# A conv norm centred on a pilot mean, three output chunks computed together, and inputs moved by 64 bytes

## The chip, the cores and the metric

The kernel runs on one core of a Trainium2 chip. The metric is the device time of one execution in microseconds (us); the time before is the median of three runs, 2594.8 (2594.53 to 2596.46). The engines are TensorE (PE, matmuls; PEld its weight loads), VectorE (DVE), ScalarE (ACT), GpSimd (POOL) and SyncE (SP), whose queue issues the DMAs.

## What is computed

Two transformer blocks on x of 256 tokens by 2048 features, fp32. Each is modulated by six vectors made from a conditioning vector c (2048 by 12288 weights per block). Only the first block's mixer is touched by the change:

```python
mod = silu(c) @ mod_w + mod_b                       # SH1, SC1, G1, SH2, SC2, G2
h = rms_norm(x, norm1_g) * (1 + sc1) + sh1
u = h @ w_in + b_in; a, gt = split(u); u = a * sigmoid(gt)      # conv_in
u = depthwise_conv(u, dw_w, width=31, causal) + dw_b
u = silu(layer_norm(u, ln_g, ln_b))                 # mean, then variance of u - mean
y = u @ w_out + b_out                               # conv_out
x = x + (1 + g1) * y
h = rms_norm(x, norm2_g) * (1 + sc2) + sh2
x = x + (1 + g2) * (square(relu(h @ w1)) @ w2)      # the MLP, d_ff = 8192
# then the second block: two kinds of attention, gates, a gated MLP, a last norm
```

## The kernel before

Features lie on the 128 partitions, in 16 blocks (KB) of 128, and the 256 tokens are the columns. Each fp32 product is made of three products in a rounded format: a number is split into a high and a low part, and high by high, low input by high weight, and high input by low weight are added in PSUM. A weight chunk (128 output features by 2048) is one DMA of 1 MB into one of four buffers `wf` (`load_w`); ACT casts each half to `wh` (L177) and DVE subtracts it for the low half `wl` (L180); two chunks of split halves can be held. `mm` (L191, L194) makes a chunk with a 512-column matmul (high weight by both parts of the input, which lie side by side) and a 256-column one; `mm_one` (L210) with three of 256 columns per block, 48 for a chunk, into half a PSUM bank. The mixer's two projections use `mm_one`, the rest `mm`.

The first block begins with SH1, SC1 and an early part of conv_in (blocks 0 to 5), bound by its DMAs, until about 140 us. Then comes the conv_in loop for blocks 6 to 15: two chunks for each, twenty turns in all. In a turn (`turn`) stand, after a chunk's matmuls: 1.1 steps of the modulation jobs G1, SC2, SH2 (`step`; a step of `mod_part_pe` loads 1 MB `wm` into one of the same four buffers and runs four matmuls, L286; sixteen of them, a transpose L293 and an addition L294 make a part), taps of the depthwise convolution, and mean rows (`into_mean`, L606: a matmul by 1/2048 that adds a finished block into the mean). The convolution of a block is done in one of three ways: on PE (`conv_pe`, L630 and L639, blocks 4, 10, 14, 15), on POOL (`conv_pool`, blocks 1, 3, 5, 7, 9, 12: ACT makes the product L654 into a ring of eight, POOL adds it L655), on DVE (`conv_dve`, the six others, 31 taps each in PSUM, L662 and L665). `TAPS` and `POOL_TAPS` say how many taps stand in a turn; two of the DVE taps stand ahead of each `wl` (`between`). What is left goes into a drain loop after the last turn (L765).

When all sixteen blocks have been added, the mean is copied (L776), subtracted from each block (L778, ten on DVE, six on POOL), and squared (L368); PE adds the squares into the variance (L369), and six steps of the modulation jobs stand between. Four rows on DVE after one on ACT (`rstd`, L337 to L342) make the reciprocal root. Up to there each engine's instructions are kept in the order of the program (`in_order`, closed by `pinned.close()`); behind it a scheduler orders them by a simulation. Then each block is multiplied by the root (L788), put through Silu (L790) and split into `s` (`uHL`), and conv_out's sixteen chunks follow, each with 1.2 steps of modulation. `flush` runs what is left of the jobs, `norm_to` makes the MLP's input, and the MLP starts with three chunks together.

Of the kernel before, what the change touches and what calls it, by code (L numbers as in the profile page):

```python
# [9 lines left out]
F32 = mybir.dt.float32  # L10
# [21 lines left out]
CONV_PACE = 1.1  # L32
LN_STEPS = 6
WOUT_PACE = 1.2
# [38 lines left out]
class Builder:  # L73
# [62 lines left out]
    def weights(self):  # L136

        a = self.a
        out = []
        for j in range(EARLY, 16):  # L140
            out += [(a["conv_in"][16 + j], 16, j not in NATIVE), (a["conv_in"][j], 16)]
        out += [(a["conv_out"][j], 16) for j in range(16)]
# [17 lines left out]
    def take(self):  # L160

        while self.plan and len(self.ahead) <= AHEAD:
            self.ahead.append(self.load_w(*self.plan.pop(0)))
        return self.ahead.pop(0)

# [222 lines left out]

    def actHL(self, tag):
        return self.big.tile([P, KB, 2, S], F32R, tag=tag, name=self.nm(tag))  # L390

# [66 lines left out]
    def build(self):  # L458
# [28 lines left out]
        nc.vector.tensor_copy(cpad[:, :, 0:1], sc[:, 0:16].unsqueeze(2))  # L487
        sel = self.keep([P, 1], "sel")
        nc.vector.memset(sel, 0.0)
# [12 lines left out]

        front = self.big.tile([P, 2 * KB * S], F32, tag="uHL", name="front")
        xn = front[:, :KB * S].rearrange("p (k t) -> p k t", t=S)
        h = self.actHL("hHL")
        a1 = self.keep([P, 16], "a1")
# [93 lines left out]
        clock = [0]  # L600
        late, summed = [], []

        def into_mean(now):
            for due, i in [t for t in late if t[0] <= now]:
                late.remove((due, i))
                nc.tensor.matmul(mean[:, :S], lhsT=self.ones_d, rhs=co[:, i], start=not summed,  # L606
                                 stop=(len(summed) == KB - 1))
                summed.append(i)

        def tap(i, j):  # L610
# [86 lines left out]
        for s in range(SLICES):  # L697
# [18 lines left out]
            else:  # L716
# [6 lines left out]
                prods = front[:, d0:d0 + NPROD * S].rearrange("p (n t) -> p n t", t=S)  # L723
                wdiag = front[:, d0 + NPROD * S:].rearrange("p (n t) -> p n t", t=4 * S)
                nc.vector.memset(us[:, :, :PAD], 0.0)
# [11 lines left out]
        self.pace(CONV_PACE)  # L737
        mean = self.aux()
# [31 lines left out]
        self.warm_rsqrt(sg[:, 0:1])  # L770

        while len(self.jobs) > 2:
            self.step(1)
        var = self.aux()
        mn = self.t1()
        nc.scalar.copy(mn, mean[:, :S])  # L776
        for kb in range(KB):
            (nc.gpsimd if kb % 8 in (2, 5, 7) else nc.vector).tensor_tensor(  # L778
                out=co[:, kb], in0=co[:, kb], in1=mn, op=ALU.subtract)
            self.sq_into(var[:, :S], co[:, kb], kb == 0, kb == KB - 1)  # L780
            if kb % 2:
                self.step(LN_STEPS / 8)
        r = self.rstd(var[:, :S])
        pinned.close()
        self.pace(WOUT_PACE)
        s = self.actHL("uHL")
        for kb in range(KB):
# [39 lines left out]
        for j in range(16):  # L827
            ps = self.mm_one(self.take(), s, KB)
            t = self.t1()
# [3 lines left out]
            self.square_sum(st[:, :S], x[:, j], j)  # L833
            self.step()
        self.flush()

# [283 lines left out]
```

## Time and profile before

| what | us |
|---|---|
| median of three runs | 2594.8 |
| the profiled execution | 2594.32 |
| its span on the core | 2592.5 |
| PE busy | 2527.7 (97%) |
| DVE busy | 1828.1 (71%) |
| ACT busy | 1323.5 (51%) |
| POOL busy | 152.1 (6%) |

The profile is of one execution; its own time stands 1.8 us above its span. A busy engine is one with an instruction under way. TensorE's matmuls are pipelined, so that the times of neighbours overlap and only the distance from start to start tells what one costs. The mean granted clock of PE over the span is 0.989 of full speed. In the rows below a tile's name stands left of the arrow and what it is made from right of it; "x10" is a count of neighbours in one row; in square brackets stands how long the engine had been idle and what released it.

### The profile page before, as it was taken

What the parts mean: (1) busy time and instruction counts of PE and PEld (TensorE: products, weight loads), DVE (VectorE), ACT (ScalarE), POOL (GpSimd) and SP (SyncE); (2) the same over time, 40 slices, a digit from 0 to 9 for tenths busy, and PEclk for the clock granted to TensorE, in tenths of its full rate; (3) what the DMA queues carried; (4) which work ended last, traced back from release to release, by engine and by line L of the source; (5) the groups of instructions that cost most, each with busy time, mean ns of one, the idle gap of its engine ahead of it and who ended that gap; (6) DMA issues with size and microseconds to landing.
All of it is one profiled execution on the core that took longest, in us unless ns stands there. A gap on an engine that the chain in (4) does not pass through costs nothing.

```text
span 2592.5 us, 38179 instructions
## 1 busy us (share of the span) xinstructions
PE 2527.7 (97%) x15340; PEld 2164.4 (83%) x15340; DVE 1828.1 (71%) x2546; ACT 1323.5 (51%) x2143; POOL 152.1 (6%) x190
## 2 busy tenths in 40 slices
PE   6999899999999999999999999999999999999997
PEld 4788668788888888887888888888788888888886
DVE  4377754777887888867976778786766556666566
ACT  4367654554554644655454554554544444444454
POOL 0068800000000000000000000000000000000000
PEclk8999999999999999999999999999999999999999
DMA  9967478778888887854654677775466666665553
GB/s 394 416 242 279 180 274 313 277 279 318 297 291 292 296 293 289 313 190 168 227 202 167 209 251 267 275 271 191 160 222 228 222 209 229 216 223 203 187 176 116
DMA packets 110338, 638.43 MB, mean 246 GB/s; under 512 B 16336, under 2 KB 16592, under 8 KB 51792
## 3 DMA queue, kind: packets, MB, share of 16 engines
q1 hardware_dynamic: 110160, 635.99, 68.7%
q8 instruction: 120, 1.97, 0.3%
q14 instruction: 58, 0.48, 0.0%
HBM read 633.85 MB, written 2.10 MB: 245 GB/s over the span
## 4 chain that ended last, share of the span: by engine, by line
PE 95%; DMA 2%; DVE 1%; ACT 1%; issue 0%; POOL 0%; SPq 0%; DVEq 0%; ACTq 0%; POOLq 0%
PE mm L191 51%; PE mm L194 27%; PE mm L210 8%; PE aux L286 2%; PE mm L573 2%; DMA slots<-in_mod_a_dram 1%; PE mm L753 1%; PE aux L530 1%; DMA front<-in_mod_a_dram 1%; PE aux L369 1%; PE mm L639 1%; PE aux L422 1%; PE aux L454 1%; PE aux L271 0%; PE aux L573 0%; DMA x<-in_xT_dram 0%
## 5 line engine op out<-in xcount | busy, mean ns | idle before, releaser
L191 PE MATMUL mm<-hHL,wh 128*128 128x512 f32 x3520 | 1243.1, 397 | 11.9 <-DVE hHL L380 11.9
L180 DVE TENSOR_TENSOR wl<-wf,wh 128x1024 fp32r<-128x1024 f32 (+1 forms) x794 | 965.9, 1219 | 356.5 <-ACT wh L177 333.6
L177 ACT CAST wh<-wf 128x1024 fp32r<-128x1024 f32 (+1 forms) x794 | 825.4, 1042 | 404.8 <-PE mm L191 240.1
L194 PE MATMUL mm<-hHL,wl 128*128 128x256 f32 x3520 | 960.9, 283 | 0.6 <-DVE wl L180 0.6
L191 PEld LDWEIGHTS mm<-hHL,wh 128*128 128x128 f32 x3520 | 652.6, 188 | 149.6 <-issue 8.9
L191 PE MATMUL mm<-uHL,wh 128*128 128x512 f32 x1984 | 691.4, 394 | 0.0
L194 PEld LDWEIGHTS mm<-hHL,wl 128*128 128x128 f32 x3520 | 663.7, 189 | 20.5 <-DVE wl L180 1.2
L194 PE MATMUL mm<-uHL,wl 128*128 128x256 f32 x1984 | 536.1, 282 | 0.0
L243 ACT COPY t<-mm 128x256 f32<-128x256 f32 x377 | 140.5, 373 | 588.2 <-PE mm L191 586.2
L191 PEld LDWEIGHTS mm<-uHL,wh 128*128 128x128 f32 x1984 | 364.5, 188 | 73.9
L194 PEld LDWEIGHTS mm<-uHL,wl 128*128 128x128 f32 x1984 | 372.9, 188 | 13.4
L265 DVE SCALAR_TENSOR_TENSOR acc<-wm,silu_c,acc 128x1024 f32<-128x1024 f32 x210 | 268.8, 1280 | 30.7 <-DMA wm<-in_w_ada_dram 26.9
L246 DVE TENSOR_TENSOR t<-mm,t 128x256 f32<-128x256 f32 x319 | 134.9, 423 | 181.1 <-ACT t L243 180.5
L655 POOL TENSOR_TENSOR room<-room,front 128x255 f32<-128x255 f32 (+9 forms) x180 | 146.6, 815 | 171.4 <-ACT front L654 158.4
L210 PE MATMUL mm<-hHL,wh 128*128 128x256 f32 x544 | 99.9, 286 | 0.0
L210 PE MATMUL mm<-uHL,wh 128*128 128x256 f32 x512 | 96.2, 288 | 0.7 <-DVE uHL L133 0.7
L210 PEld LDWEIGHTS mm<-uHL,wh 128*128 128x128 f32 x512 | 79.8, 191 | 16.4 <-issue 11.7
L210 PEld LDWEIGHTS mm<-hHL,wh 128*128 128x128 f32 x544 | 84.0, 189 | 6.9 <-issue 4.5
L191 PE MATMUL mm<-m,wh 128*128 128x512 f32 x256 | 89.5, 397 | 0.0
L665 DVE SCALAR_TENSOR_TENSOR mm<-room,vecs,mm 128x255 f32<-128x255 f32 (+9 forms) x180 | 84.7, 471 | 4.8
L654 ACT ACTIVATE front<-room,vecs 128x255 f32<-128x255 f32 (+9 forms) x180 | 74.7, 487 | 7.9 <-POOL room L655 7.9
L210 PE MATMUL mm<-hHL,wl 128*128 128x256 f32 x272 | 76.7, 282 | 0.0
(174 smaller groups left out, 1776.1 us busy)
## 6 DMA issues: line engine op xcount, KB each, us to landing
wf<-in_w_dram SPq DMA_DIRECT2D x128, 1024.0 KB, 6.7
wm<-in_w_ada_dram SPq DMA_DIRECT2D x96, 1024.0 KB, 5.2
wf<-in_win_dram SPq DMA_DIRECT2D x68, 1024.0 KB, 5.0
wm<-in_mod_w_dram SPq DMA_DIRECT2D x64, 1024.0 KB, 5.8
wf<-in_wg_dram SPq DMA_DIRECT2D x44, 1024.0 KB, 5.0
wf<-in_wu_dram SPq DMA_DIRECT2D x44, 1024.0 KB, 4.8
wf<-in_wd_dram SPq DMA_DIRECT2D x32, 896.0 KB, 4.6
slots<-in_mod_a_dram SPq DMA_DIRECT2D x22, 1024.0 KB, 15.0
```

The source lines that it names most:

```text
L177: self.nc.scalar.copy(wh, w[:, k0:k0 + n, :])
L180: self.nc.vector.tensor_tensor(out=wl, in0=w[:, k0:k0 + n, :], in1=wh, op=ALU.subtract)
L191: self.nc.tensor.matmul(ps, lhsT=h, rhs=full, start=first, stop=last, skip_group_check=True)
L194: self.nc.tensor.matmul(ps[:, :S], lhsT=l, rhs=x[:, 0, :], start=False, stop=False, skip_group_check=True)
L210: self.nc.tensor.matmul(ps[:, :S], lhsT=a, rhs=x[:, k, b], start=(k == 0 and i == 0), stop=(k == nk - 1 and i == 2))
L243: nc.scalar.copy(tb, ps[:, S:])
L246: nc.vector.tensor_tensor(out=s, in0=ps[:, :S], in1=tb, op=ALU.add)
L265: nc.vector.scalar_tensor_tensor(out=acc, in0=w[:, i], scalar=cvec[:, k + i:k + i + 1], in1=acc, op0=ALU.mult, op1=ALU.add)
L286: nc.tensor.matmul(row[32 * j:32 * j + 32, :], lhsT=cpad[:, k], rhs=w[:, j * 512:(j + 1) * 512], start=(k == 0), stop=(k == KB - 1), skip_ ...
L654: nc.scalar.activation(pr, u[:, PAD:PAD + S - s], AF.Identity, scale=tap(i, j))
L655: nc.gpsimd.tensor_tensor(out=dst[:, s:], in0=dst[:, s:], in1=pr, op=ALU.add)
L665: nc.vector.scalar_tensor_tensor(out=acc[:, s:], in0=u[:, PAD:PAD + S - s], scalar=tap(i, j), in1=acc[:, s:], op0=ALU.mult, op1=ALU.add)
```

## The change

- *Taps.* `TAPS` goes from 8 to 10 and `POOL_TAPS` from 8 to 9; block 10 moves from PE to DVE.
- *Norm.* When eight blocks are in the mean, ACT copies it, times two, into `pilot`. From then on each turn and each iteration of the drain takes up to two finished blocks, subtracts the pilot (DVE) and squares (ACT), and PE adds the square to `var`, which shares a PSUM tile with the mean. At the end dm = mean − pilot, the variance is var − dm², and dm is subtracted from the blocks (ten on DVE, six on POOL).
- *Modulation.* One step stands in each iteration of the drain, `FILL` = 6 after it, and then what is left of SC2; only SH2 is left for conv_out.
- *conv_out.* Its first three chunks are loaded without a split; four of their halves are split ahead of the normalising loop, two inside it; the three chunks' matmuls (`product`) stand in that loop, block by block, in three PSUM tiles. The next chunk is asked for at the first of the three outputs, and the order is kept by `in_order` until the third.
- *64 bytes.* `h` of the first block and `s` begin 16 floats into their buffers, which get 32 floats more; the other inputs begin where their buffers do. `sel` is kept at 32 floats.

```diff
-LN_STEPS = 6
+FILL = 6
+PILOT = 8
-PE_CONV = (4, 10, 14, 15)
+PE_CONV = (4, 14, 15)
+SHIFT = 16
+SPARE = 32
-TAPS = 8
-POOL_TAPS = 8
+TAPS = 10
+POOL_TAPS = 9
...
-    def actHL(self, tag):
-        return self.big.tile([P, KB, 2, S], F32R, tag=tag, name=self.nm(tag))
+    def actHL(self, tag, shift=0):
+        t = self.big.tile([P, KB * 2 * S + SPARE], F32R, tag=tag, name=self.nm(tag))
+        return t[:, shift:shift + KB * 2 * S].rearrange("p (k a t) -> p k a t", a=2, t=S)
...
                 summed.append(i)
+                if len(summed) == PILOT:
+                    nc.scalar.activation(pilot, mean[:, :S], AF.Identity, scale=float(KB) / PILOT)
+
+        def centre():
+            if len(summed) < PILOT or centred[1] == len(summed):
+                return
+            i = summed[centred[1]]
+            centred[1] += 1
+            nc.vector.tensor_tensor(out=co[:, i], in0=co[:, i], in1=pilot, op=ALU.subtract)
+            sq = self.t1()
+            nc.scalar.activation(sq, co[:, i], AF.Square)
+            squares.append(sq)
+
+        def into_var():
+            while squares:
+                centred[0] += 1
+                nc.tensor.matmul(var[:, :S], lhsT=self.ones_d, rhs=squares.pop(0), start=False,
+                                 stop=(centred[0] == KB), skip_group_check=True)
...
         def turn():
             clock[0] += 1
             self.step()
+            into_var()
             taps(dve=TAPS - 4, pool=POOL_TAPS, pe=1)
             into_mean(clock[0])
+            centre()
+            centre()
...
             turn()
+            if i == KB - 1:
+                first = [self.take(ahead=0)]
             glu(i, ps[:, :S], sg)
...
             taps(pe=1, dve=6, pool=4)
+            self.step(1)
             into_mean(clock[0])
+            into_var()
+            centre()
+            centre()
...
+        dm = self.t1()
+        nc.vector.scalar_tensor_tensor(out=dm, in0=pilot, scalar=-1.0, in1=mean, op0=ALU.mult, op1=ALU.add)
+        d2 = self.t1()
+        nc.vector.tensor_tensor(out=d2, in0=dm, in1=dm, op=ALU.mult)
+        v = self.t1()
+        nc.vector.tensor_tensor(out=v, in0=var, in1=d2, op=ALU.subtract)
+        self.step(FILL)
         while len(self.jobs) > 2:
             self.step(1)
-        (the copy of the mean, sixteen subtractions, squares, variance rows and six steps)
+        r = self.rstd(v)
         for kb in range(KB):
+            (nc.gpsimd if kb >= 10 else nc.vector).tensor_tensor(out=co[:, kb], in0=co[:, kb], in1=dm,
+                                                                 op=ALU.subtract)
         self.pace(WOUT_PACE)
-        s = self.actHL("uHL")
+        s = self.actHL("uHL", SHIFT)
...
+        ws = first + [self.take(), self.take(ahead=0)]
+        parts = [half(ws[0], 0), half(ws[1], 0), half(ws[2], 0), half(ws[0], 8)]
+        pss = [self.mmps() for i in range(3)]
...
             self.split(s[:, kb, 0], s[:, kb, 1], t)
+            if kb < 8:
+                for i in range(3):
+                    product(i, parts[i], kb)
+            else:
+                product(0, parts[3], kb)
+                if kb == 9:
+                    parts += [half(ws[1], 8), half(ws[2], 8)]
+                for k in {9: (), 10: (8, 9), 11: (10, 11)}.get(kb, (kb,) if kb > 11 else ()):
+                    for i in (1, 2):
+                        product(i, parts[3 + i], k)
...
-            ps = self.mm_one(self.take(), s, KB)
+            ps = pss[j] if j < 3 else self.mm_one(self.take(), s, KB)
...
             self.step()
+            if j == 0:
+                self.ask(1)
+            if j == 2:
+                pinned.close()
```

How it moves the instructions is seen at three places. First PE at the end of the mean (L606 before, L613 now). Before, the variance rows (L369) follow in pairs, with a load's matmuls (L286, `wm`) between:

```order
L606 MATMUL aux_1223<-room,ones_d 128x256 x3
L369 MATMUL aux_3242<-t_292_3246,ones_d 128x256
L369 MATMUL aux_3242<-t_293_3250,ones_d 128x256
L369 MATMUL aux_3242<-t_294_3254,ones_d 128x256
L369 MATMUL aux_3242<-t_295_3258,ones_d 128x256
L286 MATMUL aux_2752<-wm_3261,cpad 32x512 x4
L369 MATMUL aux_3242<-t_297_3268,ones_d 128x256
L369 MATMUL aux_3242<-t_298_3272,ones_d 128x256
L286 MATMUL aux_2752<-wm_3275,cpad 32x512 x4
```

Now most variance rows (L634) stand further up; behind the last two come five loads' matmuls in a row (L292), SC2's transpose (L299), and then the first of the three chunks (L844), whose high weight meets both parts of the input and whose low weight the high part:

```order
L292 MATMUL aux_2779<-wm_3296,cpad 32x512 x4
L613 MATMUL aux_1223<-room,ones_d 128x256 x2
L634 MATMUL aux_1223<-t_303_3304,ones_d 128x256
L634 MATMUL aux_1223<-t_305_3311,ones_d 128x256
L292 MATMUL aux_2779<-wm_3320,cpad 32x512 x4
L292 MATMUL aux_2779<-wm_3326,cpad 32x512 x4
L292 MATMUL aux_2779<-wm_3332,cpad 32x512 x4
L292 MATMUL aux_2779<-wm_3338,cpad 32x512 x4
L292 MATMUL aux_2779<-wm_3344,cpad 32x512 x4
L299 MATMUL aux_3352<-const,t_314_3350 128x128 x4
L844 MATMUL mm_3404<-uHL_3383,wh_3388 128x256 x2
L844 MATMUL mm_3404<-uHL_3383,wl_3389 128x256
```

What stood between the variance rows now stands in one piece ahead of conv_out, and the variance rows are gone from there. Second, DVE behind its last tap (L665 before, L692 now). Before, the subtractions of the mean (L778) and the root (L338 to L342) follow directly, then the multiplication (L788):

```order
L665 SCALAR_TENSOR_TENSOR mm_3106<-room,vecs,mm_3106 128x226
L778 TENSOR_TENSOR room<-room,t_291_3243 128x256 x10
L338 TENSOR_SCALAR t_314_3345<-aux_3242 128x256
L339 TENSOR_TENSOR t_316_3347<-t_315_3346 128x256
L340 SCALAR_TENSOR_TENSOR t_316_3347<-t_316_3347,t_314_3345 128x256
L342 SCALAR_TENSOR_TENSOR t_317_3352<-t_316_3347,t_315_3346 128x256
L788 TENSOR_TENSOR room<-room,t_317_3352 128x256 x12
L133 TENSOR_TENSOR uHL_3354<-t_319_3356,uHL_3354 128x256
```

Now the last centrings (L626) come, dm, its square and the variance (L816 to L820), then SC2's addition (L300), the root (L344 to L348), ten subtractions of dm (L826) and the first chunk's low half (L136):

```order
L626 TENSOR_TENSOR room<-room,pilot 128x256 x2
L816 SCALAR_TENSOR_TENSOR t_306_3314<-pilot,aux_1223 128x256
L818 TENSOR_TENSOR t_307_3316<-t_306_3314 128x256
L820 TENSOR_TENSOR t_308_3318<-aux_1223,t_307_3316 128x256
L300 TENSOR_TENSOR mods<-aux_3352,vecs 128x16
L344 TENSOR_SCALAR t_316_3358<-t_308_3318 128x256
L345 TENSOR_TENSOR t_318_3360<-t_317_3359 128x256
L392 SCALAR_TENSOR_TENSOR a_4620<-mods,vecs 128x16
L346 SCALAR_TENSOR_TENSOR t_318_3360<-t_318_3360,t_316_3358 128x256
L348 SCALAR_TENSOR_TENSOR t_319_3365<-t_318_3360,t_317_3359 128x256
L826 TENSOR_TENSOR room<-room,t_306_3314 128x256 x10
L136 TENSOR_TENSOR wl_3389<-wf_2973,wh_3388 128x1024
```

An addition that needs the whole of SC2 stands ahead of the root, and the subtractions behind it. Third, PE at the start of the MLP, before (L286 and L293 belong to SH2; `hHL` is the MLP's input):

```order
L286 MATMUL aux_3865<-wm_4601,cpad 32x512 x4
L286 MATMUL aux_3865<-wm_4607,cpad 32x512 x4
L293 MATMUL aux_4615<-const,t_488_4613 128x128 x4
L191 MATMUL mm_4731<-hHL_4623,wh_4520 128x512
L194 MATMUL mm_4731<-hHL_4623,wl_4521 128x256
L191 MATMUL mm_4731<-hHL_4623,wh_4520 128x512
L194 MATMUL mm_4731<-hHL_4623,wl_4521 128x256
```

and now (L370 is the last row of the norm's sum of squares):

```order
L216 MATMUL mm_4565<-uHL_3383,wl_4488 128x256
L370 MATMUL aux_3641<-t_488_4617,ones_d 128x256
L197 MATMUL mm_4730<-hHL_4622,wh_4557 128x512
L200 MATMUL mm_4730<-hHL_4622,wl_4558 128x256
L197 MATMUL mm_4731<-hHL_4622,wh_4702 128x512
L200 MATMUL mm_4731<-hHL_4622,wl_4703 128x256
L197 MATMUL mm_4730<-hHL_4622,wh_4557 128x512
L200 MATMUL mm_4730<-hHL_4622,wl_4558 128x256
```

SH2's last steps are gone from there, and two chunks (`mm_4730`, `mm_4731`) alternate from the first block, where one stood alone.

## Rows read from the trace of the kernel before

**Rows 1.** The page's part 4: the chain that ended last, by engine.

```profile
PE 95%; DMA 2%; DVE 1%; ACT 1%; issue 0%; POOL 0%; SPq 0%; DVEq 0%; ACTq 0%; POOLq 0%
```

**Rows 2.** The view by stretch, two stretches; its second line names the columns.

```profile
core 0: us, PE busy (x) PEld busy (x) DVE busy (x) ACT busy (x) POOL busy (x), PEclk, DMA share, GB/s
311.00:319.00 8.00, 1.35 (x5) 0.80 (x4) 3.13 (x7) 5.42 (x12) 6.64 (x11) 0.66 0.00 0
338.00:361.00 23.00, 19.53 (x120) 13.62 (x113) 16.78 (x40) 18.89 (x41) 0.00 (x0) 0.85 0.57 215
```

**Rows 3.** The chain of waits, end of conv_in: start us, us, what.

```profile
296.81 1.77 PE mm L630 x32
...
299.24 3.48 PE mm L639 x53
...
327.49 1.06 PE aux L369 x4
```

**Rows 4.** DVE's groups by line, conv_in loop, 140 to 297 us.

```profile
L665 DVE SCALAR_TENSOR_TENSOR mm<-room,vecs,mm 128x255 f32<-128x255 f32 (+9 forms) x149 | 70.1, 470 | 3.8
L180 DVE TENSOR_TENSOR wl<-wf,wh 128x1024 fp32r<-128x1024 f32 x36 | 48.7, 1360 | 27.6 <-ACT wh L177 27.4
```

**Rows 5.** The timeline of POOL: start us, us, engine, line, operation, count.

```profile
159.56 24.89 POOL L655 TENSOR_TENSOR room<-room,front 128x244 f32<-128x244 f32 x29
...
205.79 29.29 POOL L655 TENSOR_TENSOR room<-room,front 128x229 f32<-128x229 f32 x32 [1.44 <-ACT front L654]
...
304.12 14.31 POOL L655 TENSOR_TENSOR room<-room,front 128x245 f32<-128x245 f32 x20 [0.41 <-ACT front L654]
```

**Rows 6.** The page's part 6: DMA issues, median us to landing last.

```profile
wm<-in_mod_w_dram SPq DMA_DIRECT2D x64, 1024.0 KB, 5.8
```

**Rows 7.** The timeline from the root to the first product.

```profile
338.19 0.42 DVE L338 TENSOR_SCALAR t<-aux 128x256 f32<-128x256 f32 x1 [10.55 <-ACT t L337]
...
340.00 4.12 DVE L788 TENSOR_TENSOR room<-room,t 128x256 f32<-128x256 f32 x12
...
343.25 0.58 PE L210 MATMUL mm<-uHL,wh 128*128 128x256 f32 x1
```

**Rows 8.** The timeline of PE in conv_out, the loads' matmuls.

```profile
366.85 1.07 PE L286 MATMUL aux<-wm,cpad 128*32 128x512 f32 x8
...
380.62 1.07 PE L286 MATMUL aux<-wm,cpad 128*32 128x512 f32 x8
```

**Rows 9.** The timeline, end of conv_out and start of the MLP.

```profile
458.17 0.28 PE L210 MATMUL mm<-uHL,wl 128*128 128x256 f32 x1
...
464.38 1.07 PE L286 MATMUL aux<-wm,cpad 128*32 128x512 f32 x8 [0.77 <-DMA wm<-in_mod_w_dram]
...
466.85 0.17 DVE L294 TENSOR_TENSOR mods<-aux,vecs 128x16 f32<-128x16 f32 x1 [0.53 <-PE aux L293]
...
489.49 0.37 ACT L243 COPY t<-mm 128x256 f32<-128x256 f32 x1 [4.33 <-PE mm L191]
```

**Rows 10.** The timeline at the next seam of this kind.

```profile
1199.47 0.40 PE L191 MATMUL mm<-uHL,wh 128*128 128x512 f32 x1
...
1225.84 0.64 ACT L243 COPY t<-mm 128x256 f32<-128x256 f32 x2
```

**Rows 11.** The timeline of DVE, low halves at the MLP's start.

```profile
477.51 4.63 DVE L180 TENSOR_TENSOR wl<-wf,wh 128x1024 fp32r<-128x1024 f32 x4
```

**Rows 12.** The timeline of PE, 512-column matmuls: 13 rows with hHL, 14 with m.

```profile
1104.30 0.40 PE L191 MATMUL mm<-hHL,wh 128*128 128x512 f32 x1
...
1108.51 0.40 PE L191 MATMUL mm<-hHL,wh 128*128 128x512 f32 x1
...
1814.26 0.39 PE L191 MATMUL mm<-m,wh 128*128 128x512 f32 x1
...
1818.85 0.40 PE L191 MATMUL mm<-m,wh 128*128 128x512 f32 x1
```

**Rows 13.** The timeline of PE, 256 columns: twelve matmuls from first to last.

```profile
440.00 0.40 PE L210 MATMUL mm<-uHL,wh 128*128 128x256 f32 x2
...
441.42 0.40 PE L210 MATMUL mm<-uHL,wh 128*128 128x256 f32 x2
```

More of the change, by code (lines that the diff above doesn't have):

```diff
@@ L141, in weights @@
             out += [(a["conv_in"][16 + j], 16, j not in NATIVE), (a["conv_in"][j], 16)]
-        out += [(a["conv_out"][j], 16) for j in range(16)]
+        out += [(a["conv_out"][j], 16, j >= 3) for j in range(16)]
         for g in range(4):
@@ L158, in weights, with take, ask @@
         return out
-    def take(self):
-        while self.plan and len(self.ahead) <= AHEAD:
+    def take(self, ahead=AHEAD):
+        self.ask(ahead + 1)
+        return self.ahead.pop(0)
+    def ask(self, n):
+        while self.plan and len(self.ahead) < n:
             self.ahead.append(self.load_w(*self.plan.pop(0)))
-        return self.ahead.pop(0)
     def load_w(self, src, nk=16, parted=True):
@@ L487, in build @@
         nc.vector.tensor_copy(cpad[:, :, 0:1], sc[:, 0:16].unsqueeze(2))
-        sel = self.keep([P, 1], "sel")
+        sel = self.keep([P, 32], "sel")[:, :1]
         nc.vector.memset(sel, 0.0)
@@ L500, in build @@
         SH1, SC1, G1, SH2, SC2, G2 = range(6)
-        front = self.big.tile([P, 2 * KB * S], F32, tag="uHL", name="front")
+        front = self.big.tile([P, 2 * KB * S + SPARE], F32, tag="uHL", name="front")
         xn = front[:, :KB * S].rearrange("p (k t) -> p k t", t=S)
-        h = self.actHL("hHL")
+        h = self.actHL("hHL", SHIFT)
         a1 = self.keep([P, 16], "a1")
@@ L600, in build @@
         clock = [0]
-        late, summed = [], []
+        late, summed, squares, centred = [], [], [], [0, 0]
         def into_mean(now):
@@ L606, in into_mean @@
                 nc.tensor.matmul(mean[:, :S], lhsT=self.ones_d, rhs=co[:, i], start=not summed,
-                                 stop=(len(summed) == KB - 1))
+                                 stop=(len(summed) == KB - 1), skip_group_check=True)
                 summed.append(i)
+                if len(summed) == PILOT:
[14 more added lines that the diff above has]
+                                 stop=(centred[0] == KB), skip_group_check=True)
         def tap(i, j):
@@ L723, in build @@
                 prods = front[:, d0:d0 + NPROD * S].rearrange("p (n t) -> p n t", t=S)
-                wdiag = front[:, d0 + NPROD * S:].rearrange("p (n t) -> p n t", t=4 * S)
+                wdiag = front[:, d0 + NPROD * S:d0 + 16 * S].rearrange("p (n t) -> p n t", t=4 * S)
                 nc.vector.memset(us[:, :, :PAD], 0.0)
@@ L737, in build @@
         self.pace(CONV_PACE)
-        mean = self.aux()
+        both = self.aux()
+        mean, var = both[:, :S], both[:, S:]
+        pilot = self.tp.tile([P, S], F32, tag="rs", bufs=1, name="pilot")
         self.between = lambda: taps(dve=2)
@@ L767, in build, with half, product @@
             taps(pe=1, dve=6, pool=4)
+            self.step(1)
             into_mean(clock[0])
+            into_var()
+            centre()
+            centre()
         into_mean(1 << 20)
         self.warm_rsqrt(sg[:, 0:1])
+        while centred[0] < KB:
+            into_var()
+            centre()
+            centre()
+        dm = self.t1()
[5 more added lines that the diff above has]
+        self.step(FILL)
         while len(self.jobs) > 2:
             self.step(1)
-        var = self.aux()
-        mn = self.t1()
-        nc.scalar.copy(mn, mean[:, :S])
+        r = self.rstd(v)
         for kb in range(KB):
[L778 to L784, printed above, removed]
-        self.pace(WOUT_PACE)
-        s = self.actHL("uHL")
+            (nc.gpsimd if kb >= 10 else nc.vector).tensor_tensor(out=co[:, kb], in0=co[:, kb], in1=dm,
+                                                                 op=ALU.subtract)
+        self.pace(WOUT_PACE)
+        s = self.actHL("uHL", SHIFT)
+        def half(w, k0):
+            wh = self.sp.tile([P, 8, P], F32R, tag="wh", name=self.nm("wh"))
+            wl = self.sp.tile([P, 8, P], F32R, tag="wl", name=self.nm("wl"))
+            self.split(wh, wl, w[:, k0:k0 + 8, :])
+            return wh, wl
+        ws = first + [self.take(), self.take(ahead=0)]
+        parts = [half(ws[0], 0), half(ws[1], 0), half(ws[2], 0), half(ws[0], 8)]
+        pss = [self.mmps() for i in range(3)]
+        def product(i, part, k):
+            h, l = part[0][:, k % 8, :], part[1][:, k % 8, :]
+            for n, (w, b) in enumerate(((h, 0), (h, 1), (l, 0))):
+                nc.tensor.matmul(pss[i][:, :S], lhsT=w, rhs=s[:, k, b], start=(k == 0 and n == 0),
+                                 stop=(k == KB - 1 and n == 2))
         for kb in range(KB):
```

## The prediction

> **What bounds the kernel now.** I read the chain of waits first: 95% of the span is TensorE (PE) [rows 1]. So only PE work removed, or a place where PE stands still, moves the time. The table by stretch shows such a place: from 311 to 319 us PE works 1.35 of 8 us, at a granted clock of 0.66, and the DMA queues carry nothing; from 338 to 361 its clock is 0.85 [rows 2]. The reader should see that this is the seam between the two projections of the conv mixer. A second seam lies at the MLP's start. The rest is a solid row of matmuls, on which only the part on alignment can act. All times below are us of the profiled execution. T0 = 296.81 is where the conv_in loop's last matmul ends and block 14's convolution on PE begins [rows 3]. Everything up to the end of the MLP's first three chunks, 489.49, when ScalarE (ACT) copies the last of the three out [rows 9], is compared with the same point after the change; what follows is the same work.
>
> **Step 1, the conv_in loop.** Block 10 leaves PE: its two parts are like those of block 14, 1.77 and 3.48 us [rows 3], so 5.2 us go. Ten of the sixteen variance rows come in: two blocks took 1.06 us in the tail [rows 3], 0.53 each, so 5.3 us. They cancel. VectorE (DVE) now gives 6 taps a turn and 2 before each low half. By the counts of the loop (36 halves, 20 turns) that is 9.6 taps of 70.1/149 = 0.47, 1.8 halves of 1.36 [rows 4], half a gate and half a centring, each about as long as a tap: 7.4 of the (297 − 140) / 20 = 7.85 us that a turn lasts. It fits by 0.4, but unevenly over the turns; a stall of 0 to 3 us, and I take 1. T0' = 297.8.
>
> GpSimd (POOL) is tighter. Nine products a turn leave it 7.85 / 9 = 0.87 us each. Before, it took 29 in 24.89 (0.86) and 32 in 29.29 (0.92), but 20 in 14.31 (0.72) in the drain, where DVE only added taps in PSUM [rows 5]. "SBUF — State Buffer", section "SBUF: two separate sides", of the Trainium skill says that a DVE instruction with two SBUF inputs and a GpSimd one shut each other out for a whole instruction; the 0.72 against 0.92, and low halves of 1.36 in the loop, agree with it. By that rule the ten centrings in the loop (two SBUF inputs) would hold POOL for some 4 us more. I keep it for the rival below.
>
> **Step 2, from T0' to the first product of conv_out.** Before, that took 46.4 us, to 343.25 [rows 7]. Now eleven loads of SC2 remain after T0', each of 1 MB, and DVE's order puts SC2's last addition in front of the reciprocal root (the second piece of order above), so the products wait for the loads. Three buffers serve them, since the first conv_out chunk holds the fourth. Three loads are under way at T0'; every later one waits for the matmuls of the load three before it, and lands 5.8 after its issue [rows 6]. On PE these matmuls are queued behind blocks 14 and 15 (5.2 each) and the last two means, which wait for DVE's last tap, about T0' + 20 (31 taps of 0.47, eight centrings, two weight diagonals). If nothing else is late, the last two loads are issued at T0' + 22 and 24 and consumed by T0' + 30. If ACT, whose copies for block 14 stand behind nine products, waits out a POOL backlog of up to 8, it is T0' + 38. I take T0' + 35, nearer the late end, since POOL has no slack in step 1: 332.8. Then:
> - from the end of the last load's matmuls to the addition, 466.85 + 0.17 less 464.38 + 1.07 = 1.6 [rows 9]: 334.4
> - four DVE rows of the root, 338.19 to 340.00 = 1.8 [rows 7]: 336.2
> - ten subtractions at 4.12 / 12 = 0.34 [rows 7]: 339.6
> - four low halves, 4.6 [rows 11]: 344.2
> - multiply, table load, Silu, split: 343.25 − 340.00 = 3.25 [rows 7]: 347.5, which is 4.2 later than before.
>
> The sixteen subtractions and square rows that stood in the tail are hidden by the loads; were the loads early, the chain would still hold DVE's 20 us of taps, so the cover is worth at most the 30 to 38 just bounded.
>
> **Step 3, three chunks together.** 144 matmuls at 1.42 / 12 = 0.118 [rows 13] are 17.0. The second halves of chunks 2 and 3 can be split only once the first halves of chunk 1 are done, at block 9: two casts and two low halves, which the two late blocks of chunk 1 cover in part; 0 to 4, I take 2. The restart runs at a lower clock, as the 0.85 of 338 to 361 shows: 15% of the first 15 us or so, 2.3. So 347.5 + 21.3 = 368.8. Before, the third chunk was done at 366.85, where its load's matmuls follow [rows 8]: 1.9 sooner. The normalising loop was PE's pace before and costs little; now it is covered, but later.
>
> **Step 4, thirteen chunks.** A chunk with one load's matmuls takes (380.62 − 366.85) / 2 = 6.89 [rows 8], thirteen 89.5; three more loads of SH2 at 1.07 [rows 9] are 3.2: 461.5. Before, the last matmul of conv_out ended at 458.17 + 0.28 = 458.45 [rows 9], and five loads' matmuls still lay behind it.
>
> **Step 5, the seam to the MLP.** Before, 458.45 to 489.49: 31.0, with the last load's wait and its matmuls until 465.45 [rows 9] and only one weight chunk split, so that four low halves stand at 477.51 [rows 11]. After, no load stands there and two chunks are interleaved from the first block. Then it should be like the next seam of this kind, 1199.87 to 1225.84 = 26.0 [rows 10]. 461.5 + 26.0 = 487.5, against 489.49: 2.0 sooner.
>
> **Step 6, 64 bytes.** 2160 matmuls of 256 columns (by the code 33 chunks of 48 in the two projections and 12 of 48 in the early one) read inputs moved by 64 bytes against the weights. No row shows such a pair. The nearest are the 512/256 pairs: (1108.51 − 1104.30) / 12 = 0.351 with hHL, in phase with its weights, (1818.85 − 1814.26) / 13 = 0.353 with m, 64 bytes off [rows 12]. The difference of 2.3 ns per pair may belong to either matmul and, for the 256 columns, to either sign: ± 2.3 ns × 2160 = ± 5 us. No reason excludes a side; I take 0. The spare bytes also move every buffer, but inputs of the 5760 pairs (360 full chunks of 16) stay where they were relative to weights in steps of 128 bytes: 0, bounded by ± 2.3 ns × 5760 = ± 13 us.
>
> The sum is −2.0 on 2594.3 (the span of 2592.5 and 1.8 around it); the median of the runs is 0.5 above that execution: 2592.8, so 2593.
>
> **The rivals.**
> - Slower: POOL can't take nine products a turn. At 0.92 each a turn lasts 8.3; ACT's casts wait behind its products, and once the one chunk of lead is gone PE waits 0.4 × 20 = 8 us in the loop. It decides from a mean spacing above 0.87. For it: the 0.92; against: the 0.86, and POOL ends sooner afterwards. 2593 + 8 = 2601.
> - Faster: POOL keeps up, the loads are done at T0' + 30 (−5), no late halves (−2) and a shorter clock ramp (−1.5): 2584.5. For it: the queues are idle from 311 to 319, so that transfers that wait for nothing but buffers have room; against: three buffers.
> - The phase is worth something by itself, −3 ns or so: −5 to −8, 2586; or the whole layout is worse, +8 to +13, 2604. Rows 12 show that 64 bytes matter by 0.7% at all.
> - A floor is gone. Matmuls of 256 columns are 118.3 ns apart [rows 13], which is more than 256 columns at 2.4 GHz, the full granted clock, would take (106.7). If the phase alone kept them there, up to 2160 × 11.6 ns = 25 us would go: 2568. "TensorE: Matmul & The Clock Gate", section "Back-to-back issue gap", of the Trainium skill gives the columns at 2.4 GHz and 2.5 ns, 109.2, for such a matmul by itself, and says that a stream with weight loads is set by both; by it the gain would be 20 us. The pairs with m, off phase, are no faster, which speaks against the floor.
>
> **How the numbers follow.** Runs differ by 0.1%, and about 0.2%, 5.2 us, is what can be told from no change. The forecast has 0.42, POOL's rival 0.20, the faster chain 0.20, a gain by phase or layout 0.09, a worse layout 0.04, the floor 0.05. Faster is 0.34 (0.20 + 0.09 + 0.05), slower 0.24, the rest 0.42. The range, 2581 to 2603, holds POOL's rival and the faster chain with some spread, and leaves out the floor and most of the bad layout.
>
> **What would show it.** Step 1: PE busy through the loop and its end within 2 us of 297.8; a gap before conv_in matmuls that ends with ACT or DVE would show the rival. Step 2: the last load's matmuls at 328 to 336, then the addition of SC2, the root and ten subtractions in a row on DVE, first product near 347.5. Step 3: three tiles alternating, 21 us. Step 5: 26 us. Step 6: the spacing of 118.3 ns and that of the pairs, either moved. The prediction is wrong if the spacing moves by over 2 ns, if the first product comes before 342 or after 353, or if a stretch after 490 changes.

## The result, and the profile after

The changed kernel takes 2618.41 us (median of four runs, 2617.36 to 2619.08) against 2594.66 before: a ratio of 1.0090, with a 95% interval of 1.0072 to 1.0107. It is 23.8 us slower; 2593 with a range to 2603 was forecast. The chain of the profile after shows at once that PE no longer sets the time as it did in [rows 1]:

```profile
PE 90%; DMA 3%; DVE 3%; ACT 2%; POOL 1%; issue 0%; SPq 0%; POOLq 0%; DVEq 0%; ACTq 0%
```

The table below gives, for the kernels of this study, when the work came past five places. The loop's end is the end of the last modulation matmul ahead of block 14's convolution; the first product is the start of conv_out's first matmul; then come the ends of its third and of its sixteenth chunk, of the 48th pair of the MLP (three chunks), and of the span. Each is the start or end of one matmul record of that kernel's profile, counted from the start of its span.

| us | loop end | first product | third chunk | conv_out | MLP's three | span |
|---|---|---|---|---|---|---|
| before | 296.8 | 343.3 | 366.9 | 458.5 | 489.8 | 2592.5 |
| after | 304.9 | 358.2 | 390.8 | 484.1 | 511.9 | 2617.3 |
| e1_pool8 | 297.2 | 354.0 | 386.6 | 479.9 | 507.4 | 2612.9 |
| e2_dve8 | 305.0 | 379.1 | 411.7 | 498.8 | 526.6 | 2631.2 |
| e3_norm_ahead | 304.0 | 356.4 | 386.4 | 479.7 | 507.4 | 2612.0 |
| e4_fill_late | 303.4 | 345.5 | 378.1 | 486.2 | 513.8 | 2618.3 |
| e5_noshift | 304.6 | 357.1 | 389.7 | 484.2 | 511.7 | 2616.8 |
| e6_before_phase | 297.5 | 344.2 | 367.5 | 456.4 | 487.8 | 2590.5 |
| e7_skew | 303.1 | 354.9 | 378.4 | 471.6 | 499.6 | 2604.5 |
| e8_taps_skew_root | 296.9 | 349.6 | 374.1 | 466.3 | 493.8 | 2598.2 |
| e9_fill1_layout | 298.0 | 346.2 | 368.9 | 464.4 | 491.9 | 2594.4 |
| e10_layout | 306.0 | 358.7 | 391.3 | 482.2 | 510.3 | 2613.3 |

The differences of neighbouring columns, after less before, make up the 24.8 us between the two spans, but for rounding: the end of the conv_in loop +8.1, from there to the first product +6.8, the three chunks +8.9 (32.6 for 23.7), the other thirteen +1.8, the seam to the MLP −3.6, and all that follows +2.7. The loop itself lasted 10.0 us longer, since its first chunk started 1.9 us sooner in the profile after (138.3, for 140.2 before). Over the twelve profiles that start lies between 137.9 and 140.2; why is open.

The loop first. POOL's additions, which answer to [rows 5], now stand almost without a gap:

```profile
149.92 69.78 POOL L682 TENSOR_TENSOR room<-room,front 128x251 f32<-128x251 f32 x77
...
247.83 38.66 POOL L682 TENSOR_TENSOR room<-room,front 128x237 f32<-128x237 f32 x45 [2.43 <-ACT front L681]
```

77 in 69.78 are 0.91 us each. Twenty turns from 138.3 to 304.9 are 8.33 us each, nine times 0.93. The chain runs over POOL here, from a product of ACT through additions, back into a product, and then into the cast of a weight half (start, us, what):

```profile
193.44 1.52 ACT front L681 x4
195.00 0.60 POOL room L682
...
212.20 0.49 ACT front L681
213.05 0.94 ACT wh L183
214.02 1.39 DVE wl L186
```

PE feels it at two places. Its waits from 140 to 305 us were one of 0.2 us before; now they are these (us in total, times, longest):

```profile
PE aux L299 <- ACT t L296: 5.9, 1, 5.9
PE aux L292 <- DMA wm<-in_mod_w_dram: 4.0, 1, 4.0
```

The 4.0 us, until 225.4, are for a modulation load that was issued at 218.1, behind the weight halves of the chain above. The 5.9 us, until 268.7, are for ACT's copy ahead of the transpose of G1. That copy stands behind products that wait for POOL, and then behind instructions that are themselves part of the change: the pilot, and the squares of two blocks that wait for DVE's centrings (`in_order` keeps ACT to that order):

```profile
263.87 0.28 ACT pilot L618
264.17 1.29 DVE room L626 x2
265.48 0.42 ACT t L628
...
266.25 1.88 ACT wh L183 x2
268.13 0.49 ACT t L296
```

After each of the two stops PE first goes on at a granted clock of 0.50 (225.3 to 230.0, and 268.6 to 271.0). The view by stretch shows the second stop, in the first row, which before was

```profile
240.00:280.00 40.00, 40.00 (x335) 33.76 (x334) 29.87 (x50) 29.50 (x60) 36.16 (x45) 1.00 0.64 230
```

and then PE nearly still at the seam, at half clock (a granted clock of 0.50, 1.2 GHz), while the DMA engines too are idle for 44% of that time:

```profile
240.00:280.00 40.00, 34.07 (x241) 28.66 (x240) 32.78 (x59) 28.94 (x61) 34.36 (x43) 0.91 0.51 185
340.00:360.00 20.00, 5.03 (x23) 2.54 (x20) 10.58 (x23) 8.14 (x11) 0.00 (x0) 0.50 0.56 209
360.00:380.00 20.00, 13.96 (x74) 11.34 (x73) 9.42 (x21) 10.96 (x21) 0.00 (x0) 0.84 0.08 26
```

The columns are those of [rows 2]. The chain of the seam, which answers to [rows 3, 7], shows what stands there:

```profile
334.30 7.74 DMA wm<-in_mod_w_dram
...
342.09 1.98 PE aux L292 x8
...
345.88 0.17 DVE mods L300
...
347.76 3.10 DVE room L826 x9
350.86 4.54 DVE wl L136 x4
...
355.82 1.28 ACT L850
357.12 0.61 ACT t L850
357.75 0.41 ACT uHL L135
...
358.18 0.42 DVE uHL L136
358.61 0.35 DVE room L848
...
358.98 0.61 ACT t L850
```

First the last loads of SC2, then its addition, the root, the subtractions and the low halves, as step 2 had them. Behind them a round of four that repeats: Silu on ACT (0.61), cast on ACT (0.41), subtraction on DVE (0.42), the next block's multiplication on DVE (0.35), 1.86 us from Silu to Silu. At full clock PE does the nine matmuls of a block in 1.1 us and waits for the next; in the first three blocks and again behind the second halves, at a granted clock of 0.50, they stand 0.213 us apart and take about as long as the round.

### The profile page after: what moved, and what is told of

Its sections match the earlier page's. It is cut to its first block, busy times and chain, and to the rows that moved or that the text cites. A ratio compares the mean times of both kernels' runs of the same rounds, so it can differ in the third digit from the quotient of the medians.

```text
span 2617.3 us, 38011 instructions
## 1 busy us (share of the span) xinstructions
PE 2528.2 (97%) x15244; PEld 2163.3 (83%) x15244; DVE 1850.2 (71%) x2595; ACT 1327.1 (51%) x2141; POOL 151.3 (6%) x190
## 4 chain that ended last, share of the span: by engine, by line
PE 90%; DMA 3%; DVE 3%; ACT 2%; POOL 1%; issue 0%; SPq 0%; POOLq 0%; DVEq 0%; ACTq 0%
PE mm L197 51%; PE mm L200 26%; PE mm L216 5%; DMA slots<-in_mod_a_dram 2%; PE mm L580 2%; PE aux L292 1%; POOL room L682 1%; DMA wm<-in_mod_w_dram 1%; PE aux L537 1%; DMA front<-in_mod_a_dram 1%; PE mm L785 1%; PE aux L429 1%; PE aux L461 1%; DVE wl L186 0%; PE aux L277 0%
## 5 line engine op out<-in xcount | busy, mean ns | idle before, releaser
L197 PEld LDWEIGHTS mm<-uHL,wh 128*128 128x128 f32 x1984 | 364.7, 188 | 78.1 <-DVE uHL L136 0.3
L271 DVE SCALAR_TENSOR_TENSOR acc<-wm,silu_c,acc 128x1024 f32<-128x1024 f32 x210 | 268.7, 1280 | 27.5 <-DMA wm<-in_w_ada_dram 17.9
L692 DVE SCALAR_TENSOR_TENSOR mm<-room,vecs,mm 128x255 f32<-128x255 f32 (+14 forms) x210 | 98.9, 471 | 5.9
L681 ACT ACTIVATE front<-room,vecs 128x255 f32<-128x255 f32 (+9 forms) x180 | 77.0, 488 | 14.1 <-POOL room L682 14.0
L216 PE MATMUL mm<-uHL,wh 128*128 128x256 f32 x416 | 75.9, 282 | 0.0
L216 PEld LDWEIGHTS mm<-uHL,wh 128*128 128x128 f32 x416 | 63.9, 188 | 8.4 <-issue 6.7
```

The costliest lines, as they stand in the source:

```text
L197: self.nc.tensor.matmul(ps, lhsT=h, rhs=full, start=first, stop=last, skip_group_check=True)
L216: self.nc.tensor.matmul(ps[:, :S], lhsT=a, rhs=x[:, k, b], start=(k == 0 and i == 0), stop=(k == nk - 1 and i == 2))
L271: nc.vector.scalar_tensor_tensor(out=acc, in0=w[:, i], scalar=cvec[:, k + i:k + i + 1], in1=acc, op0=ALU.mult, op1=ALU.add)
L681: nc.scalar.activation(pr, u[:, PAD:PAD + S - s], AF.Identity, scale=tap(i, j))
L692: nc.vector.scalar_tensor_tensor(out=acc[:, s:], in0=u[:, PAD:PAD + S - s], scalar=tap(i, j), in1=acc[:, s:], op0=ALU.mult, op1=ALU.add)
```

## The experiments

**e1_pool8 and e2_dve8**: which of the two engines that got more taps sets the loop.

```diff
-POOL_TAPS = 9
+POOL_TAPS = 8
```

> The changed kernel with POOL_TAPS back at 8; nothing else. Theory (POOL sets the turn): nine additions at 0.92 us are 8.3 us, and ACT's weight casts stand behind the products that wait for POOL; with eight a turn is 7.9 us again, the last modulation matmuls of the conv_in loop end at about 297 instead of 304.9 us, and the kernel takes about 2612. Rival (DVE's ten taps and the centrings set the turn): the loop ends at 303 or later, 2617.

```diff
-TAPS = 10
+TAPS = 8
```

> The changed kernel with TAPS back at 8, so that DVE has two taps fewer in each turn and more in the drain; POOL keeps nine. Theory (POOL sets the turn): the loop still ends at 303 to 305 us, and the drain gets longer by DVE's left-over taps (about 40 x 0.5 = 20 us at most, part of it behind the loads), 2620 to 2635. Rival (DVE sets the turn): the loop ends at about 297 us.

Measured: with eight products for POOL the loop ends at 297.2, with DVE relieved instead at 305.0 as in the changed kernel. So POOL's ninth product costs most of the 8 us, 7.7. That the ten taps of DVE fit is not shown: in e1 PE still stops once, for the same copy,

```profile
PE aux L299 <- ACT t L296: 4.7, 1, 4.7
```

and the chain to that stop runs over DVE's taps until 240.7, where ACT finishes a block that it waited for, and only then over products and additions of POOL. The 816 matmuls that the 64 bytes made 4.5 ns shorter (the layout runs below), 3.7 us, make up for most of it. With both counts back at eight (e8) one stop of 0.9 is left. e1 takes 2614.71 us in its one run, 2.7 more than its theory said: of the 7.7 gained in the loop, 3.5 are given back ahead of the first product (56.8 us behind the loop's end, 53.3 in the changed kernel). The chain in this drain runs over DVE's taps until 321.7, and then over products left over for POOL until 325.0. e2 takes 2633.01 in one run: what DVE doesn't do in the loop it does in the drain, on the path.

**e3_norm_ahead and e7_skew**: what holds the three chunks at 32.6 us.

```diff
+        def normed(kb):
             nc.vector.tensor_tensor(out=co[:, kb], in0=co[:, kb], in1=r, op=ALU.mult)
             t = self.t1()
             nc.scalar.activation(t, co[:, kb], AF.Silu, scale=self.vec("conv_ln_g", kb),
                                  bias=self.vec("conv_ln_b", kb))
+            return t
...
+        ts = [normed(0), normed(1)]
         for kb in range(KB):
-            self.split(s[:, kb, 0], s[:, kb, 1], t)
+            if kb + 2 < KB:
+                ts.append(normed(kb + 2))
+            self.split(s[:, kb, 0], s[:, kb, 1], ts[kb])
```

> The changed kernel, with the multiplication and Silu of the normalising loop written two blocks ahead of the split. Theory (kept in program order, multiply, Silu, cast and subtraction of a block run one after the other over DVE and ACT, 1.86 us a block): the three chunks take about 22 us instead of 32.6 and the kernel about 2607. Rival (the second weight halves and the half clock hold the three chunks): they still take 29 us or more, 2614 or more.

Measured: 30.0 us, 2613.74 in one run. By the numbers this is the rival's result, but for the first ten blocks the chain does not run over weights or PE; it does so only from 371.95 on:

```profile
357.21 0.60 ACT t L850
357.81 0.30 ACT uHL L135
...
358.13 0.43 DVE uHL L136
358.56 0.34 DVE room L848
...
358.93 0.60 ACT t L850
...
371.95 0.96 ACT wh L135
...
376.61 9.82 PE mm L844 x66
```

The round is still there, 1.72 us: ACT puts block k + 2 through Silu ahead of the cast of block k, and DVE multiplies k + 3 behind the subtraction of k, which waits for that cast. So the cast must stand ahead of the next Silu, with the multiplications two blocks ahead (`scaled_by_r` and `silu` are the two halves of `normed`):

```diff
+        scaled_by_r(0)
+        scaled_by_r(1)
+        ts = [silu(0)]
         for kb in range(KB):
+            if kb + 2 < KB:
+                scaled_by_r(kb + 2)
+            nc.scalar.copy(s[:, kb, 0], ts[kb])
+            if kb + 1 < KB:
+                ts.append(silu(kb + 1))
+            nc.vector.tensor_tensor(out=s[:, kb, 1], in0=ts[kb], in1=s[:, kb, 0], op=ALU.subtract)
```

> The changed kernel with the normalising loop skewed: DVE multiplies two blocks ahead, ACT casts a block before it puts the next through Silu. Two blocks ahead with Silu in front of the cast still went round DVE and ACT once per block, 1.72 us. Theory (the loop's order is what holds the three chunks): ACT needs 0.9 us a block, less than PE; the three chunks take 22 to 25 us instead of 32.6, and the kernel 2609 to 2611. Rival (the second halves of the weights and the half clock): 28 us or more, 2613 or more.

Measured: the three chunks take 23.5 us, and the kernel 2606.25 in one run, 3 us below its forecast (in it the loop ends 1.8 us sooner and the first product follows 1.5 us sooner than in the changed kernel, which its edit does not touch). Now PE's own matmuls are the chain, but for one stop for the second halves of the weights, from 364.96 to 369.15, two casts and two low halves:

```profile
354.86 10.10 PE mm L844 x65
...
364.98 1.06 ACT wh L135
...
367.20 1.22 DVE wl L136
...
369.15 9.25 PE mm L844 x65
```

The order of the loop was worth 9.1 us, as much as the 8.9 that the three chunks had lost; the stop of 4.2 remains inside.

**e4_fill_late**: whether the loads of SC2 hold the root.

```diff
-        self.step(FILL)
-        while len(self.jobs) > 2:
-            self.step(1)
         r = self.rstd(v)
...
                     for i in (1, 2):
                         product(i, parts[3 + i], k)
+        self.step(FILL)
+        while len(self.jobs) > 2:
+            self.step(1)
+        self.pace(WOUT_PACE)
```

> The changed kernel with the FILL steps moved behind the normalising loop, so that the reciprocal root stands ahead of SC2's addition on DVE. Theory (SC2's loads hold the root back): the first product of conv_out comes about 10 us sooner after the loop's end (43 instead of 53 us), the loads' matmuls then cost about 6 us behind the three chunks; 2610 to 2614. Rival (the loads of the two further weight chunks or DVE's taps are as late): the first product stays at 50 us or more after the loop's end, 2617 to 2623.

Measured: 2620.10 in one run, 6 us or more above the theory's time. The first product comes 42.1 us after the loop's end instead of 53.3, as the theory said. But conv_out's other thirteen chunks then take 108.0 us instead of 93.3: the loads stand in front of the fourth chunk's weights in the queue, and PE waits for both, 6.2 us in all where the changed kernel has no wait. The chain behind the three chunks:

```profile
378.14 2.76 PE aux L292 x24
380.91 8.18 DMA wf<-in_conv_out_dram
389.11 1.05 ACT wh L183
```

So the loads of SC2 did hold the root, and moved away they are paid elsewhere.

**e5_noshift, e6_before_phase, e10_layout**: the 64 bytes, and the spare bytes.

```diff
-SHIFT = 16
+SHIFT = 0
```

> The changed kernel with SHIFT = 0: the spare bytes stay, the two inputs lie at the start of their buffers. In the changed kernel the 256-column matmuls stand 114.3 ns apart with hHL and 117.8 with uHL, where they had 118.8 before, and the 512/256 pairs with uHL take 352.0 ns, where they had 350.9. Theory (the 64 bytes give the faster 256-column matmuls, the spare bytes the slower pairs): 118.8 for both, pairs still 352.0; about 4 us slower than the changed kernel, 2622, less where other engines set the conv_in loop. Rival (the place of the buffers in steps of more than 64 bytes decides): 114 to 115 ns stay.

e6 is the kernel before with `h` and `s` 64 bytes into buffers that have 512 bytes more:

```diff
+SHIFT = 16
+SPARE = 128
...
-        return self.big.tile([P, KB, 2, S], F32R, tag=tag, name=self.nm(tag))
+        t = self.big.tile([P, KB * 2 * S + (0 if tag == "m" else SPARE)], F32R, tag=tag, name=self.nm(tag))
+        return t[:, shift:shift + KB * 2 * S].rearrange("p (k a t) -> p k a t", a=2, t=S)
```

> The kernel before with the 64 bytes alone: h of the first block and s begin 16 floats into buffers with 128 floats more, so that all other inputs keep their places relative to the weights in steps of 512 bytes. Theory (the 64 bytes are worth 4.5 ns on each matmul with h in the conv_in loop, 1.5 ns in the early part and 0.9 with s): 3.7 + 0.8 + 0.7 = 5 us less where PE is the bound, 2590, pairs unchanged at 350.7, 350.9 and 353.0 ns. Rival (the gain belongs to the other layout): 118 ns, no change.

e10 is the changed kernel with the same buffers:

```diff
-SPARE = 32
+SPARE = 128
-        sel = self.keep([P, 32], "sel")[:, :1]
+        sel = self.keep([P, 1], "sel")
```

> The changed kernel with the spare bytes changed alone: 128 floats instead of 32 in the two shifted buffers, none in the third, sel one float again, so that the relations of before hold in steps of 512 bytes but for the 64. Theory (the spare bytes slow the 512/256 pairs with uHL and take most of the gain on s): pairs with uHL 350.9 instead of 352.0 ns (1984 of them, 2.1 us), 256-column matmuls with s 114.3 instead of 117.8 (624 on the path, 2.2 us), pairs with m 353.0 instead of 351.4; about 4 us less than the changed kernel, 2614. Rival (it was the order of the work, not the place): no change in these.

Measured, as the mean distance from start to start in ns over all neighbouring records of a kind without a gap (592 to 783 of them for the 256 columns, 1687 pairs with uHL, 222 with m):

| | before | after | e5 | e6 | e10 |
|---|---|---|---|---|---|
| 256 columns, h in the loop | 118.8 | 114.3 | 118.6 | 114.6 | 115.1 |
| 256 columns, s | 118.8 | 117.8 | 119.8 | 114.3 | 113.6 |
| pairs with uHL | 350.9 | 352.0 | 352.0 | 350.9 | 350.9 |
| pairs with m | 353.0 | 351.4 | 351.4 | 353.0 | 353.0 |

For the distances the theories hold: the shift makes the 256-column matmuls faster, the spare bytes alone make the pairs with uHL slower (and those with m faster), and with spare bytes in steps of 512 s gains 4.5 (e6) to 5.2 ns (e10) where the change gave it 1.0. What e6 shows of twelve such matmuls, for [rows 13]: 440.43 − 439.07 = 1.36 us, 113.3 ns each:

```profile
439.07 0.39 PE L212 MATMUL mm<-uHL,wh 128*128 128x256 f32 x2
...
440.43 0.39 PE L212 MATMUL mm<-uHL,wh 128*128 128x256 f32 x2
```

In time, e5 is as slow as the changed kernel (2618.58 in one run, 0.2 more than its median, where 4 were expected): slower matmuls leave less to wait for, and PE's two stops in the loop are 7.8 us there against 9.9. e10 takes 2615.15, 1.0078 of before (1.0064 to 1.0091), and its span behind the MLP's first three chunks is 2103.0 us, as before's 2102.7, against 2105.4 after. The eight profiles with 32 spare floats have 2104.4 to 2105.6 there, the four others 2102.5 to 2103.0. So the +2.7 belongs to the layout; 1984 pairs with uHL at 1.1 ns are 2.2 of it. e6 takes 2589.56 against 2595.13 of before on the same chip, 0.9979 (0.9970 to 0.9988): it beats both kernels. Its profiled execution, at 2592.28, is one of the slower of its eleven runs; it places 2.6 us of gain in conv_out (88.9 us for the last thirteen chunks and their loads, 91.5 before), and the loop does not end sooner in it: PE waits there for two modulation loads, 2.7 us, which it did not before. Where the rest of the 5.6 us lies in the faster executions is open.

**e8_taps_skew_root**: three parts mended together (TAPS and POOL_TAPS 8, block 10 on PE, the loop of e7, and this):

```diff
-        self.step(FILL)
-        while len(self.jobs) > 2:
-            self.step(1)
         r = self.rstd(v)
...
+        self.step(FILL)
+        while len(self.jobs) > 2:
+            self.step(1)
         self.pace(WOUT_PACE)
```

> The changed kernel with three parts mended: taps as before (TAPS and POOL_TAPS 8, block 10 on PE), the skewed normalising loop, and the reciprocal root and the subtractions of dm written ahead of the FILL steps, whose loads' matmuls stay where they were on PE. Theory (these three are where the time went): the conv_in loop ends at 294 to 297 us, the first product comes 44 us later instead of 53, the three chunks take 23 us, the MLP's first group ends near 485; 2587 to 2591. Rival (the loads of SC2 and of the two weight chunks hold the products whatever stands on DVE): first product 50 us or more after the loop, 2594 or more.

Measured: 2601.10, a ratio of 1.0023 (1.0014 to 1.0032) to before. The loop ends at 296.9 and the three chunks take 24.5, but the first product comes 52.7 us after the loop, not 44: this part of the theory falls, and the time is the rival's. Behind DVE's last tap the chain runs over loads, first of SC2, then of a weight chunk, whatever stands on DVE:

```profile
330.23 5.70 DMA wm<-in_mod_w_dram
...
335.98 1.98 PE aux L292 x8
337.98 5.39 DMA wf<-in_conv_out_dram
343.39 1.05 ACT wh L135
```

**e9_fill1_layout**: e8 with the buffers of e10, and five steps taken out of that place.

```diff
-FILL = 6
-WOUT_PACE = 1.2
+FILL = 1
+WOUT_PACE = 1.6
```

> The mended kernel of the run before this one (taps as before, skewed normalising loop, root ahead of FILL) with FILL = 1 in place of 6, five more modulation steps spread over conv_out (WOUT_PACE 1.6), and the layout that keeps the unshifted inputs in place in steps of 512 bytes (128 spare floats in two buffers). Theory (SC2's loads and the two weight chunks, through three buffers, held the first product at 349.4 us): it comes at 343 to 345; conv_out gets 5 us longer by the five steps; the pairs with uHL are back at 350.9 ns and the 256-column matmuls with s at 114.3: 2589 to 2594. Rival (DVE's taps and centrings hold it): first product at 348 or later, 2595 or more.

Measured: 2597.55, 1.0011 of before (1.0002 to 1.0020). The time is the rival's (2595 or more). The first product comes at 346.2, 48.3 after the loop's end, between what the two said: the loads are off the chain, and DVE is what remains, whose last tap now ends at 326.7 (at 314.3 in the kernel before) and behind which all the rest stands in a row:

```profile
326.23 0.47 DVE mm L692
...
335.26 3.62 DVE room L823 x9
338.89 4.54 DVE wl L136 x4
```

So two waits of nearly one length lie over each other there, the loads' and DVE's.

## Why the prediction was wrong, step by step

The forecast point for the MLP's first three chunks was 487.5, against 489.49 before. That row is not the copy of the last of the three, as the prediction has it (another follows at 492.28), and it stands 0.3 us ahead of the end of the 48th pair, 489.8. For the table's place the forecast is thus 487.8. It came at 511.9, and the rest took 2.7 more. By steps: loop +7.1, first product +3.6, three chunks +11.3, thirteen chunks +0.6, seam +1.5. All three signs of being wrong that the prediction names came: the spacing moved by 4.5 ns, the first product came after 353, and a stretch after 490 changed.

- **Step 3 failed, and cost most.** "The normalising loop was PE's pace before and costs little; now it is covered, but later" was wrong. The step counted PE's matmuls, the weights and the clock, and not the loop that feeds them. Before, that loop stood behind `pinned.close()`, and a scheduler had put twelve multiplications in a row ahead (L788 x12 in [rows 7]); the change moves `pinned.close()` behind conv_out's third output, so that the order of the text is the order of the engines, and in the text each block's four instructions follow each other. e7 shows it: 9.1 us. The line stood in the diff. Of the other two terms, the second halves cost 4.2 in e7 (0 to 4, with 2 taken), and the three chunks then took 23.5 for 21.3, so that the sum of 17.0 and 2.3 holds.
- **Step 1 failed by the engine it counted, not by POOL's price.** "It fits by 0.4 ... a stall of 0 to 3 us, and I take 1" was worked out for DVE's turn. PE stopped for 9.9 us, and both stops end a chain through ACT, which the step did not count: its casts and copies stand behind products that wait for POOL, and the last stop also behind the pilot and the squares. For POOL the rival's sum, a turn of 8.3 us and 8 us in all, is what came (8.33, and the loop's end 8.1 later), with e1 as proof that the ninth product costs most of it. That the sum fits so closely is in part luck: the loop itself lasted 10.0 longer, it began 1.9 sooner, the faster matmuls took 3.7 off, and PE went on at half clock after each stop, none of which is in the sum. It had a chance of 0.20, although [rows 5] showed 0.92 in a stretch where POOL hardly waited, and the change takes POOL's slack. The rule of the Trainium skill ("SBUF — State Buffer", "SBUF: two separate sides"), that a DVE instruction with two SBUF inputs and a GpSimd one shut each other out, agrees with the 0.91 of the profile after; no run here separates that lock from other causes.
- **Step 2 was mis-sized in one term**: the last SC2 matmuls ended 39.1 us after the loop, where 35 was taken from 30 to 38. The five terms behind it came to 14.1 us (14.7 forecast). e4, e8 and e9 show that it was a bound with a second one just beneath: loads, then DVE's taps and centrings.
- **Step 4** was right: 93.3 for 92.7.
- **Step 5**, 26.0 forecast, or 26.3 to the table's place, was 27.8. ACT casts a weight half ahead of the last output's evacuation, which then starts 0.9 us after the last matmul's end, where before it followed at once (the matmul ended at 458.45). Before and after:

```profile
458.49 0.47 ACT L830 ACTIVATE t<-mm,vecs 128x256 f32<-128x256 f32 x1 [4.40 <-PE mm L210]
```

```profile
484.11 1.04 ACT L183 CAST wh<-wf 128x1024 fp32r<-128x1024 f32 x1 [3.04 <-PE mm L216]
485.06 0.47 ACT L900 ACTIVATE t<-mm,vecs 128x256 f32<-128x256 f32 x1
```

- **Step 6** took 0 for both parts. The phase itself is worth 4.5 ns a matmul, 0.21% or 5.6 us of the kernel when alone (e6), as much as the bound of 5 us; in the changed kernel PE waited in the loop for other engines, the distance with s fell by 1.0 only, and the layout took 2.7 us back behind the MLP's first chunks. So a move of whole steps of 128 bytes, put at 0, was not nothing.
- **The range** took each rival alone. POOL and the three chunks are independent (e1 mends the one and leaves the other at 32.6, e7 the reverse), and both came: 7.1 + 11.3 is more than any single case. That a loop kept in program order costs more was no case at all.

## What to carry to other kernels

Where a change extends a stretch that is kept in program order, write down the round that each engine makes in it, instruction by instruction: a loop whose stages alternate between two engines runs at the sum of its stages unless the text is skewed. An engine that is 6% busy over the span can be nearly full where it works; divide its work by the stage, and trust the slow stretch of its row. Then follow who stands behind it in program order: in the loop here PE never waited for POOL itself, but for ACT and for a load. And an instruction moved out of a wait gains only down to the next wait beneath it (here loads through three buffers, then DVE), which should be priced before the first is taken away.

## What the runs showed of the hardware

The distance of matmuls depends on where the moving input starts, beyond steps of 128 bytes. With the starts of the buffers in the built programs, input less weights modulo 512 bytes: the 256-column matmuls stand 118.6 to 118.8 ns apart at 128 and 384, 119.8 at 256, 117.8 at 320, 113.6 to 115.1 at 192 and 114.3 at 448; the 512/256 pairs take 350.6 to 350.9 at 128 and 384, 352.0 at 256, 351.4 at 64 and 353.0 at 192. Places 256 bytes apart (128 and 384, 192 and 448) agree. So the 64 bytes help one kind of matmul (118.8 to 114.3, 3.8%), while the pairs are slowest (353.0 for 350.9, 0.6%) at the same place, 192, though there they were seen with m alone; and 32 spare floats are enough to move all of it. No run moved the weights by themselves, so that the input's own place instead of its distance from the weights is not excluded. Within a kernel the distance also changes between chunks (48 in 5.46 or 5.65 us in the loop of e1 and of the changed kernel); why is open.
